# A written order made with other model costs: longer fixed times for VectorE, ScalarE and GpSimd, more time per matmul, a higher backlog limit

## The chip, the cores and the metric

One NeuronCore of a Trainium2 chip runs the whole program. The metric is device microseconds of one execution. The core has TensorE (matmuls and transposes, PE in the profile, with its weight loads under PEld), VectorE (DVE), ScalarE (ACT), GpSimd (POOL) and SyncE (SP, which issues DMAs). Each engine works through its own instructions in the order in which they were written, and waits at semaphores for the others.

## The reference

One layer of a streaming encoder. 1088 tokens (1024 of a new stream and 64 of a running one) of width 1024 pass through:

```
h   = rmsnorm(x) * (1 + sc1) + sh1            # sc, sh, g: silu(c) @ w_ada + b_ada
z   = h @ w_in                                # retention q,k,v,gate; GLA q,k,v,gate; decays
o_r = retention(q, k, v, state)               # 4 heads of 128, chunks with a carried state
o_r = groupnorm(o_r) * g_ret_norm * silu(gate)
o_g = gla(q, k, v, log_a, state)              # 4 heads of 64, decay per channel
o_g = rms(o_g) * g_gla_norm * silu(gate)
x   = x + g1 * (concat(o_r, o_g) @ w_out)
h2  = rmsnorm(x) * (1 + sc2) + sh2
a, up = h2 @ w_ffn_in                         # 2 x 2816
x   = x + g2 * ((silu(conv3(a) + conv_b) * up) @ w_ffn_out);  y = rmsnorm(x)
```

The states of both mixers and the last rows of the convolution are outputs too. All of it is float32.

## The kernel before

Activations lie transposed, with the width on the partitions and tokens along the free axis, in three blocks `c` of 384, 384 and 320 tokens (`CW` is 384, `WID` has the three). The projections of `w_in` (`proj`, `proj2`, `vproj`) are the main work of TensorE. Every operand is split into a high and a low part, and a product is three matmuls: high by high, low by high, high by low (`mm3`, L242). In the trace these main matmuls write tile `mm`, and read `act_hi`, `act_lo` and the split weights `hi`, `lo`. The weight's low part is a VectorE subtraction, `lo<-raw,hi`.

Beside the projections run generators, one for each piece of side work: `gla(p, c0)` for two pairs of GLA heads, `ret(hd, ...)` for four retention heads (L1227), tails that normalize an output (`gla_tail`, `ret_tail`), `decays`, and `mod_pieces`, which computes a part of the modulation on VectorE, ScalarE and GpSimd. Nothing runs them on the chip: they run while the program is written, and so set the order of the instructions. After each triple of main matmuls `flow.tick()` (L124) steps every generator whose time has come. Model time `flow.t` advances only when a matmul or a transpose is written (`mm`, L233, and `tr`, L238). A generator yields the delay after which it wants to go on. Many delays hold `behind()`: each `Engine` (L75 to 98) keeps a model of when it is done, `busy`, to which every operation adds a fixed time and its elements over a rate, and `behind()` is how far that lies ahead of model time. So larger costs of an engine make a generator that waits for it wait for more main matmuls.

Where a stage must be over before the next may begin, `flow.drain` or `flow.until` advance model time without main matmuls: what side work is left then is written with nothing of the projections in between.

A GLA chunk of a pair of heads is: score matmuls of the block itself (`sc<-q,k`, on VectorE `att`), seven levels (operands `qbd` and `kk` from VectorE, ScalarE and GpSimd, one group of score matmuls, and VectorE's sum into `att`), a transpose of `kh`, and three output steps (`o<-...`, state update `sbd` on VectorE). Three chunks follow each other for each pair. Its tail takes sums of squares, a root on VectorE, a scale `on` on ScalarE, and transposes.

A retention chunk is: three score matmuls, `ratt` (VectorE's mask), a transpose of k scaled on ScalarE to `kz`, three output steps (with VectorE's new state `rstate`, the sum `on` and its statistics), and its tail: `rsqrt_steps` (L329, eleven small VectorE instructions `ri`, `rj`, `ra`, `rr`), the scale `on<-on,bmv,rr`, three transposes `sc<-ident,on`, and the product into `mix`. Head 3's gate projection is the last one of the attention. As its blocks finish, `split_mix(c)` (L1346) splits the eight `mix` tiles of block c for the output projection: ScalarE casts `act_hi`, and GpSimd and VectorE subtract `act_lo` by turns. The output projection writes tile `dX`, and VectorE takes it up in `ab`.

`mod_piece` (L529) goes on only when `V.behind()` is not over `VECTOR_LIMIT`:

```
while V.behind() > VECTOR_LIMIT or S.behind() > SCALAR_LIMIT:
    yield 0.3
```

Of the kernel before, what the change touches and what calls it, by code (L numbers as in the profile page):

```python
# [13 lines left out]
F32R = mybir.dt.float32r  # L14
# [50 lines left out]
LOADS_AT = 9.0  # L65
RET_TAIL = 1.0
GLA_TAIL = 2.0
VECTOR_LIMIT = 1.0
SCALAR_LIMIT = 2.0
LEVEL_LIMIT = 1.0  # L70
OUT_LIMIT = 1.0
# [122 lines left out]
def stream_step_kernel(  # L194
# [7 lines left out]
    nc = tc.nc  # L202
    ctx.enter_context(tc.manual_schedule())
    flow = Flow()
    T = nc.tensor
    V = Engine(flow, nc.vector, 960.0, 0.08)
    S = Engine(flow, nc.scalar, 1200.0, 0.09)
    G = Engine(flow, nc.gpsimd, 470.0, 0.09)

    const = ctx.enter_context(tc.tile_pool(name="const", bufs=1))  # L210
    act_ctx, early_ctx, psum_ctx = ExitStack(), ExitStack(), ExitStack()
# [14 lines left out]
    ones = const.tile([P, 1], F32, name="ones")  # L226
    G.memset(ones, 1.0)

# [4 lines left out]
    def mm(out, lhsT, rhs, start, stop, more=False):  # L233
        T.matmul(out, lhsT, rhs, start=start, stop=stop, skip_group_check=more)  # L234
        n = int(np.prod(rhs.shape[1:]))
        flow.t += max(n / 2400 + 0.0025, 0.108) if rhs.dtype == F32R else max(n / 600, 0.213)

    def tr(out, in_, n=P):  # L238
        T.transpose(out=out, in_=in_, identity=ident[0:n, 0:n])
# [2 lines left out]
    def mm3(out, trip, first=True, last=True, tick=True):  # L242
        n = len(trip)
        for i, (sh, sl, mh, ml) in enumerate(trip):
            mm(out, sh, mh, first and i == 0, False)
            mm(out, sh, ml, False, False)
            mm(out, sl, mh, False, last and i == n - 1)
            if tick and i < n - 1:
                flow.tick()
# [27 lines left out]
    def split_unit():  # L277
# [4 lines left out]
        lo = wp.tile([P, nk, ncol], F32R, tag="lo", name="lo", bufs=3)  # L282
        S.copy(out=hi, in_=raw)

        def low(eng=V):
            eng.tensor_tensor(out=lo, in0=raw, in1=hi.bitcast(F32), op=ALU.subtract)
            used[0] = True
# [41 lines left out]
    def rsqrt_steps(v, n, tag, out, w=P):  # L329
        ii = smallp[0].tile([P, n], I32, tag=tag + "i", name=tag + "i", bufs=2)[0:w]  # L330
        V.tensor_scalar(out=ii, in0=v.bitcast(I32), scalar1=1, scalar2=None,
                        op0=ALU.logical_shift_right)
        yield
        jj = smallp[0].tile([P, n], I32, tag=tag + "j", name=tag + "j", bufs=2)[0:w]
        V.tensor_scalar(out=jj, in0=ii, scalar1=-1, scalar2=0x5F3759DF,
                        op0=ALU.mult, op1=ALU.add)
        r = jj.bitcast(F32)
        for it in range(3):
            V.busy += 0.36
            yield  # L340
            a = smallp[0].tile([P, n], F32, tag=f"{tag}a", name=tag + "a", bufs=2)[0:w]
            V.scalar_tensor_tensor(out=a, in0=v, scalar=-0.5, in1=r, op0=ALU.mult, op1=ALU.mult)
            yield
            V.tensor_tensor(out=a, in0=a, in1=r, op=ALU.mult)
            yield
            r2 = smallp[0].tile([P, n], F32, tag=f"{tag}r", name=tag + "r", bufs=3)[0:w]
            V.scalar_tensor_tensor(out=r2, in0=a, scalar=1.5, in1=r, op0=ALU.add, op1=ALU.mult)
            r = r2
        out.append(r)

    def rsqrt(v, n, tag, w=P):
        out = []
        for _ in rsqrt_steps(v, n, tag, out, w):
            pass
        return out[0]
# [12 lines left out]
    def load_x(t):  # L368
# [3 lines left out]
        else:  # L372
            G.memset(xt[SMP:P, :], 0.0)
            nc.sync.dma_start(out=xt[0:SMP, :], in_=x_sample[0])
# [14 lines left out]
    for i, (name, src, n) in enumerate((  # L389
# [3 lines left out]
        if i % 2 == 0 and i < 6:  # L393
# [8 lines left out]
    T.transpose(out=pv[:, 0:16], in_=cr, identity=ident[0:16, 0:16])  # L402
    S.activation(out=csil.rearrange("p k j -> p j k"),
                 in_=pv[:, 0:16].rearrange("p (j k) -> p j k", j=2), func=AF.Silu)
# [41 lines left out]
    def norm_sum(c, j):  # L446
        if c not in ssqs:
            ssqs[c] = small.tile([P, 3], F32, tag="ssq", name="ssq", bufs=3)
        junk = qkp.tile([P, D], mybir.dt.bfloat16, tag="gt", name="junk", bufs=2)
        S.activation(out=junk, in_=xs[c * 3 + j], func=AF.Square, accum_out=ssqs[c][:, j:j + 1])  # L450

    def norm_steps(c):
        vv = small.tile([P, 3], F32, tag="vv", name="vv", bufs=3)
        V.tensor_scalar(out=vv, in0=ssqs[c], scalar1=1.0 / D, scalar2=EPS, op0=ALU.mult,
                        op1=ALU.add)
        out = []
        yield
        yield from rsqrt_steps(vv, 3, "n", out)
        rstds[c] = out[0]

    def norm_scale(c, j, eng):
        x, r = xs[c * 3 + j], rstds[c][:, j:j + 1]
        if eng is S:
            S.activation(out=x, in_=x, func=AF.Copy, scale=r)
        else:
            eng.tensor_scalar(out=x, in0=x, scalar1=r, scalar2=None, op0=ALU.mult)

    c4 = const.tile([P, KD, 4], F32R, name="c4")
    S.copy(out=c4[:, :, 0:2], in_=csil)
    V.tensor_tensor(out=c4[:, :, 2:4], in0=csil, in1=c4[:, :, 0:2].bitcast(F32), op=ALU.subtract)  # L470
# [58 lines left out]
    def mod_piece(which, dst, q, loads):  # L529
        accs = [attn.tile([P, 512], F32, tag=f"acc{j}", name=f"acc{j}", bufs=1) for j in range(2)]  # L530
        for kk in range(0, KD, 2):
# [3 lines left out]
            for i in range(2):  # L535
                for j in range(2):
                    while V.behind() > VECTOR_LIMIT or S.behind() > SCALAR_LIMIT:
                        yield 0.3
                    if j and phase[0] == "ret":
# [3 lines left out]
                        else:  # L543
                            pr = qkp.tile([P, 512], F32, tag="gt", name="prod", bufs=2)
                            S.activation(out=pr, in_=raw[:, i, :], func=AF.Copy,
                                         scale=csil[:, kk + i, 1:2])
                            G.tensor_tensor(out=accs[1], in0=accs[1], in1=pr, op=ALU.add)
                    else:
# [88 lines left out]
    def h_hi(c, k):  # L637
        h[c][k] = act_pair()
        S.copy(out=h[c][k][0], in_=hw[c, k])

    def h_lo(c, k, eng):
        hh, hl = h[c][k]
        eng.tensor_tensor(out=hl, in0=hw[c, k], in1=hh.bitcast(F32), op=ALU.subtract)

    def make_h(c, k):
        h_turn(c, k)
        h_mod(c, k, V)
        h_hi(c, k)
        h_lo(c, k, G)

# [29 lines left out]
    def ev_gla(p, name, scale):  # L680
# [3 lines left out]
        def f(c, w, ps):  # L684
            t = slots.get()
            if w < CW:
                G.memset(t[:, w:CW], 0.0)
            S.mul(out=t[:, 0:w], in_=ps[:, 0:w], mul=scale)
# [3 lines left out]
    def gate_gla(m):  # L692
        def f(c, w, ps):
# [7 lines left out]
            else:  # L701
                V.scalar_tensor_tensor(out=gt[:, 0:w], in0=gt[:, 0:w], scalar=1.0,
                                       in1=ps[:, 0:w], op0=ALU.add, op1=ALU.mult)
                G.tensor_tensor(out=mt[:, 0:w], in0=mt[:, 0:w], in1=gt[:, 0:w], op=ALU.mult)
        return f
# [414 lines left out]
    def gla_tail(p, c, on, ss):  # L1120
        w = WID[c]
        ms = small.tile([P, 6], F32, tag="ms", name="ms", bufs=2)
        V.tensor_scalar(out=ms, in0=ss, scalar1=1.0 / P, scalar2=EPS, op0=ALU.mult, op1=ALU.add)
        rs = []
        for _ in rsqrt_steps(ms, 6, "g", rs):
            yield 0.2
        rs = rs[0]
        yield 0.2
        for j in range(3):
            for hd in range(2):  # L1130
                i = 2 * j + hd
                S.activation(out=on[:, j, hd, :], in_=on[:, j, hd, :], func=AF.Copy,
                             scale=rs[:, i:i + 1])
        yield max(S.behind(), 0.0) + GLA_TAIL
        for hd in range(2):
            pt = bank(ps_sc, "sc")
            for j in range(3):
                tr(pt[:, j * P:(j + 1) * P], on[:, j, hd, :])
            m = 2 * p + hd
            mt = mix[c][4 + m]  # L1140
            if mt is None:
                mt = mix[c][4 + m] = mxg.tile([P, CW], F32, tag="mx", name="mix", bufs=12)
                S.activation(out=mt[:, 0:w], in_=pt[:, 0:w], func=AF.Copy, scale=ghalf[:, m:m + 1])
            else:
                V.scalar_tensor_tensor(out=mt[:, 0:w], in0=pt[:, 0:w], scalar=ghalf[:, m:m + 1],
                                       in1=mt[:, 0:w], op0=ALU.mult, op1=ALU.mult)
            if hd == 1:
                ons.free()
            yield 1.0
# [1211 lines left out]
```

## Time and profile before

| what | us |
|---|---|
| median of 3 runs (1485.37 to 1487.78) | 1486.16 |
| profiled execution | 1485.04 |
| its span | 1483.2 |
| start of the GLA stage, of retention, of the output projection | about 105, 331, 600 |
| TensorE busy | 1364.4 (92% of the span) |
| VectorE busy | 1071.6 (72%) |
| ScalarE, GpSimd busy | 625.4 (42%), 308.9 (21%) |
| mean granted clock of TensorE | 0.979 of full speed |

The profile lists busy time, and for an engine's idle time the work that ended it. A window row gives the busy time of each engine in a stretch of the span, with the number of instructions, and the granted clock: 1.00 is 2.4 GHz, 0.50 is 1.2 GHz. In a row of waits stand the waiting group, the releaser, the sum, the number and the largest. Nearly every side operation is recorded at line 91 (the `Engine` helper) and every matmul at 234 or 239, so groups are told apart by the names of their tiles.

### The profile page before, as it was taken

Reading aid. Unit: us, or ns where it says so; the run is one execution under the profiler, and the core shown is the slowest. Engines: PE = TensorE matmul, PEld = TensorE weight load, DVE = VectorE, ACT = ScalarE, POOL = GpSimd, SP = SyncE. Lnnn points to the kernel's source line nnn. Section 1 sums busy time; section 2 is a strip of 40 time slices with the busy share of each in tenths; the row PEclk is TensorE's granted clock in tenths of the full one; section 3 lists DMA queues with packets and bytes.
Section 4 is the critical chain, followed back from the end, with each engine's and each line's share of the span. In section 5 each row is a group of like instructions: output and inputs, shape, how many; then the busy total and the mean of one; then the engine's idle time right before and its main releaser. Section 6 shows DMA issues by size and latency. Waiting matters only on the chain.

```text
span 1483.2 us, 23803 instructions
## 1 busy us (share of the span) xinstructions
PE 1364.4 (92%) x9082; PEld 1270.0 (86%) x9082; DVE 1071.6 (72%) x1992; ACT 625.4 (42%) x1277; POOL 308.9 (21%) x412
## 2 busy tenths in 40 slices
PE   5998888989989998899779999999999999899996
PEld 3788777879989998899779999999999997788875
DVE  6637878966886788756697777777777765568775
ACT  5635434432333223545454444444434444334343
POOL 3334433425342423411101000000000011100010
PEclk9999999999999999999889999999999999999999
DMA  8420102123223222444212332233223338555522
GB/s 261 150 78 2 58 15 64 57 85 101 90 73 90 81 68 74 139 139 145 81 39 83 107 101 61 83 107 107 93 93 107 107 112 283 189 196 184 174 78 114
DMA packets 157977, 158.27 MB, mean 107 GB/s; under 512 B 9738, under 2 KB 128616, under 8 KB 157864
## 3 DMA queue, kind: packets, MB, share of 16 engines
q1 hardware_dynamic: 147303, 120.58, 26.4%
q0 software_dynamic: 10560, 36.18, 7.0%
q8 instruction: 71, 1.16, 0.3%
q14 instruction: 43, 0.34, 0.1%
HBM read 126.80 MB, written 29.93 MB: 106 GB/s over the span
## 4 chain that ended last, share of the span: by engine, by line
PE 53%; DVE 23%; issue 8%; ACT 7%; DMA 2%; POOL 1%; DVEq 0%; ACTq 0%; POOLq 0%
PE dX L234 22%; PE mm L234 10%; PE dA L234 8%; PE mn L234 5%; PE al L234 3%; PE o L234 2%; DVE lo L91 2%; DMA rb<-d_y 2%; DVE qbd L91 2%; DVE att L91 2%; ACT hi L91 2%; DVE ab L91 1%; DVE acc L91 1%; DVE cv L91 1%; DVE X L91 1%
## 5 line engine op out<-in xcount | busy, mean ns | idle before, releaser
L234 PE MATMUL dX<-X,lo 128*128 128x272 f32 x1344 | 180.8, 290 | 4.8 <-DVE ab L91 2.1
L234 PE MATMUL dX<-X,hi 128*128 128x272 f32 x1296 | 175.2, 292 | 6.1 <-DVE ab L91 2.7
L234 PEld LDWEIGHTS dX<-X,lo 128*128 128x128 f32 x1344 | 174.2, 190 | 6.2 <-ACT X L91 2.1
L234 PEld LDWEIGHTS dX<-X,hi 128*128 128x128 f32 x1296 | 169.1, 191 | 6.9 <-issue 2.9
L234 PE MATMUL mm<-act_hi,hi 128*128 128x384 f32 (+1 forms) x480 | 170.7, 356 | 0.3 <-DVE mix L91 0.2
L234 PE MATMUL mm<-act_lo,hi 128*128 128x384 f32 (+1 forms) x480 | 158.8, 331 | 0.1
L234 PE MATMUL mm<-act_hi,lo 128*128 128x384 f32 (+1 forms) x480 | 158.4, 330 | 0.0
L91 ACT CAST hi<-raw 128x512 fp32r<-128x512 f32 (+1 forms) x116 | 91.1, 787 | 78.5 <-DVE raw L91 66.9
L234 PE MATMUL al<-ba,hi 128*128 128x512 f32 x396 | 101.7, 400 | 4.5 <-DVE x L91 4.5
L234 PE MATMUL mn<-lo,hi 128*128 128x512 f32 x396 | 94.8, 396 | 2.7 <-ACT lo L91 2.1
L234 PEld LDWEIGHTS mm<-act_hi,hi 128*128 128x128 f32 x480 | 92.0, 192 | 1.9 <-DVE mix L91 0.5
L234 PEld LDWEIGHTS mm<-act_lo,hi 128*128 128x128 f32 x480 | 91.9, 191 | 0.7 <-POOL act_lo L91 0.3
L234 PEld LDWEIGHTS mn<-lo,hi 128*128 128x128 f32 x396 | 74.8, 190 | 19.4 <-ACT lo L91 2.6
L234 PEld LDWEIGHTS mm<-act_hi,lo 128*128 128x128 f32 x480 | 91.3, 190 | 0.0
L91 DVE SCALAR_TENSOR_TENSOR cv<-ab,cw,cv 128x1088 f32<-128x1088 f32 x44 | 59.3, 1348 | 44.3 <-ACT cv L91 44.3
L234 PEld LDWEIGHTS al<-ba,hi 128*128 128x128 f32 x396 | 71.9, 190 | 19.6 <-DVE x L91 5.6
L234 PE MATMUL mm<-hi,act_hi 128*128 128x256 f32 x288 | 87.3, 303 | 0.2 <-ACT hi L91 0.2
L234 PE MATMUL mm<-lo,act_hi 128*128 128x256 f32 x288 | 82.1, 285 | 2.5 <-DVE lo L91 2.5
L234 PE MATMUL mm<-hi,act_lo 128*128 128x256 f32 x288 | 81.6, 283 | 0.0
L91 POOL TENSOR_TENSOR acc<-acc,prod 128x512 f32<-128x512 f32 x42 | 64.3, 1530 | 78.2 <-ACT prod L91 77.4
L234 PE MATMUL dX<-act_hi,hi 128*128 128x384 f32 (+1 forms) x192 | 66.6, 347 | 8.8 <-DVE ab L91 4.4
L234 PE MATMUL dA<-X,hi 128*128 128x272 f32 x552 | 74.4, 291 | 0.0
(354 smaller groups left out, 3086.4 us busy)
## 6 DMA issues: line engine op xcount, KB each, us to landing
raw<-in_w_ffn_in_dram SPq DMA_DIRECT2D x44, 512.0 KB, 3.8
raw<-in_w_ada_dram SPq DMA_DIRECT2D x32, 512.0 KB, 4.1
raw<-in_w_in_dram SPq DMA_DIRECT2D x28, 512.0 KB, 3.7
rw<-in_w_ffn_out_dram SPq DMA_DIRECT2D x51, 256.0 KB, 3.4
d_y<-cv POOLq DMA_DIRECT2D x22, 512.0 KB, 4.9
rb<-d_y POOLq DMA_DIRECT2D x44, 256.0 KB, 3.8
raw<-in_w_out_dram SPq DMA_DIRECT2D x18, 512.0 KB, 4.3
wa<-in_w_ada_dram SPq DMA_DIRECT2D x16, 512.0 KB, 5.0
```

Source lines behind the costliest of these rows:

```text
L91: return call(*args, **kw)
L234: T.matmul(out, lhsT, rhs, start=start, stop=stop, skip_group_check=more)
```

## The change

The model costs of the engines are raised (fixed time of an operation from 0.08 to 0.25 us on VectorE, from 0.09 to 0.2 on ScalarE and GpSimd), a matmul is taken to last 0.011 us longer in the fast form (unless it is at the floor of 0.108) and 0.222 at least in the other, the extra 0.36 in the root's steps is taken out, and the limit of VectorE's backlog for `mod_piece` is 1.5 instead of 1.0. None of these lines issues anything; they set the order in which the rest is written.

```diff
-VECTOR_LIMIT = 1.0
+VECTOR_LIMIT = 1.5
...
-    V = Engine(flow, nc.vector, 960.0, 0.08)
-    S = Engine(flow, nc.scalar, 1200.0, 0.09)
-    G = Engine(flow, nc.gpsimd, 470.0, 0.09)
+    V = Engine(flow, nc.vector, 960.0, 0.25)
+    S = Engine(flow, nc.scalar, 1200.0, 0.2)
+    G = Engine(flow, nc.gpsimd, 470.0, 0.2)
...
     def mm(out, lhsT, rhs, start, stop, more=False):
...
-        flow.t += max(n / 2400 + 0.0025, 0.108) if rhs.dtype == F32R else max(n / 600, 0.213)
+        flow.t += max(n / 2400 + 0.0135, 0.108) if rhs.dtype == F32R else max(n / 600, 0.222)
...
         for it in range(3):
-            V.busy += 0.36
             yield
```

The order is the same up to about 105 us, and again from the output projection's normalization on. Three places show what moves between.

TensorE, third chunk of the second GLA pair, from its fifth level to the first output step, before (`sc<-qbd,kk` are the levels, `mm` the main matmuls, `sc<-ident,on` transposes of an earlier chunk's output):

```order
L234 MATMUL sc<-qbd_1077,kk 128x128 x3
L239 MATMUL sc<-ident,on 128x128 x3
L234 MATMUL mm<-act_hi,hi 128x384
L234 MATMUL mm<-act_lo,hi 128x384
L234 MATMUL mm<-act_hi,lo 128x384
L234 MATMUL sc<-qbd_1079,kk 128x128 x3
L234 MATMUL mm<-act_hi,hi 128x384
L234 MATMUL mm<-act_lo,hi 128x384
L234 MATMUL mm<-act_hi,lo 128x384
L234 MATMUL o<-sbd_1083,qe 128x256
L234 MATMUL o<-v,att 128x128 x2
L234 MATMUL o<-v,khT 128x256
```

The same place after:

```order
L234 MATMUL sc<-qbd_1077,kk 128x128 x3
L239 MATMUL sc<-ident,kh 128x128 x3
L239 MATMUL sc<-ident,on 128x128 x6
L234 MATMUL sc<-qbd_1079,kk 128x128 x3
L234 MATMUL sc<-qbd_1075,kk 128x128 x3
L234 MATMUL sc<-qbd_1077,kk 128x128 x3
L234 MATMUL sc<-qbd_1079,kk 128x128 x3
L234 MATMUL o<-sbd_1083,qe 128x256
L234 MATMUL o<-v,att 128x128 x2
L234 MATMUL o<-v,khT 128x256
```

No main matmul is left between the levels and output steps there; they stand in the chunk before, which has 159 of them instead of 108.

VectorE, retention head 1, last output steps of its second chunk, before (`on<-on,bmv,rr` is the scale of the first chunk's output):

```order
L91 SCALAR_TENSOR_TENSOR rstate<-rstate,o 128x128
L91 SCALAR_TENSOR_TENSOR on<-o,txi,on 128x128
L91 BN_STATS bst<-on 128x6
L91 BN_AGGR bmv<-bst 128x2
L91 SCALAR_TENSOR_TENSOR ra<-ve,rr 128x3
L91 SCALAR_TENSOR_TENSOR acc_4357<-raw,csil,acc_4357 128x512
L91 TENSOR_TENSOR ra<-ra,rr 128x3
L91 SCALAR_TENSOR_TENSOR rr<-ra,rr 128x3
L91 TENSOR_TENSOR ratt<-sc,tdec 128x384
L91 TENSOR_SCALAR on<-on,bmv,rr 128x128 x3
```

The same place after:

```order
L91 SCALAR_TENSOR_TENSOR ra<-ve,rr 128x3
L91 TENSOR_TENSOR ra<-ra,rr 128x3
L91 SCALAR_TENSOR_TENSOR rr<-ra,rr 128x3
L91 TENSOR_SCALAR on<-on,bmv,rr 128x128 x3
L91 TENSOR_TENSOR lo<-raw,hi 128x1024
L91 SCALAR_TENSOR_TENSOR rstate<-rstate,o 128x128
L91 SCALAR_TENSOR_TENSOR on<-o,txi,on 128x128
L91 BN_STATS bst<-on 128x6
L91 BN_AGGR bmv<-bst 128x2
L91 TENSOR_REDUCE msum<-st 128x4
L91 TENSOR_TENSOR ratt<-sc,tdec 128x384
```

The scale stands ahead of the third output step instead of behind it, and behind no `ratt`.

VectorE, end of the attention, from the last head's last output step on, before (`rstate<-smp,o` is the last state, `msum` belongs to the modulation):

```order
L91 SCALAR_TENSOR_TENSOR rstate<-smp,o 128x128
L91 SCALAR_TENSOR_TENSOR on<-o,txi,on 128x128
L91 BN_STATS bst<-on 128x6
L91 BN_AGGR bmv<-bst 128x2
L91 TENSOR_TENSOR lo<-raw,hi 128x1024
```

The same place after:

```order
L91 TENSOR_TENSOR act_lo<-mix,act_hi 128x384 x4
L91 SCALAR_TENSOR_TENSOR rstate<-smp,o 128x128
L91 SCALAR_TENSOR_TENSOR on<-o,txi,on 128x128
L91 BN_STATS bst<-on 128x6
L91 BN_AGGR bmv<-bst 128x2
L91 SCALAR_TENSOR_TENSOR mix<-sc,v_122,mix 128x384
L91 TENSOR_SCALAR ve<-bmv 128x3
L91 TENSOR_SCALAR ri<-ve 128x3
L91 TENSOR_SCALAR rj<-ri 128x3
L91 TENSOR_TENSOR act_lo<-mix,act_hi 128x384 x4
```

The subtractions `act_lo` of the first two blocks now stand around the last output step and ahead of the rest of its tail; before they follow the tail's scale. On TensorE 9 main matmuls lie between the last output step with its transposes and the tail's transposes, where there were 51.

## Rows read from the trace of the kernel before

**Rows 1.** The page: busy time, share of the span and instructions of each engine.

```profile
PE 1364.4 (92%) x9082; PEld 1270.0 (86%) x9082; DVE 1071.6 (72%) x1992; ACT 625.4 (42%) x1277; POOL 308.9 (21%) x412
```

**Rows 2.** Windows of GLA and retention: busy by engine, granted clock, DMA share.

```profile
core 0: us, PE busy (x) PEld busy (x) DVE busy (x) ACT busy (x) POOL busy (x), PEclk, DMA share, GB/s
130.00:331.00 201.00, 170.95 (x1157) 156.20 (x1156) 166.86 (x343) 80.67 (x269) 76.75 (x81) 0.98 0.17 51
331.00:592.00 261.00, 240.22 (x1653) 234.14 (x1652) 199.81 (x491) 81.10 (x156) 93.95 (x74) 0.99 0.27 82
```

**Rows 3.** Waits of TensorE, 130 to 331 us: sum, number, largest.

```profile
PE sc L234 <- DVE att L91: 14.3, 13, 3.7
```

**Rows 4.** Waits of TensorE, 331 to 592 us.

```profile
PE sc L239 <- DVE on L91: 10.2, 5, 3.1
PE o L234 <- DVE rstate L91: 4.7, 5, 1.5
PE o L234 <- DVE ratt L91: 3.7, 3, 1.4
```

**Rows 5.** Windows of level stretches, first and last of six.

```profile
137.50:158.70 21.20, 18.79 (x120) 18.22 (x120) 19.55 (x32) 7.70 (x20) 12.28 (x12) 0.92 0.16 46
291.40:313.00 21.60, 17.49 (x114) 15.49 (x113) 19.01 (x41) 7.54 (x22) 9.91 (x10) 1.00 0.05 19
```

**Rows 6.** Windows of whole GLA chunks, the last the stage's tail.

```profile
137.30:167.10 29.80, 26.39 (x169) 24.76 (x170) 25.22 (x45) 11.39 (x37) 12.28 (x12) 0.94 0.18 55
197.90:230.90 33.00, 28.40 (x197) 25.68 (x196) 28.84 (x58) 14.52 (x47) 13.36 (x16) 1.00 0.16 50
230.90:259.60 28.70, 23.73 (x174) 22.39 (x172) 23.07 (x51) 9.62 (x35) 10.91 (x13) 0.94 0.09 26
259.60:289.00 29.40, 26.74 (x196) 24.62 (x195) 26.41 (x55) 13.53 (x47) 11.63 (x12) 1.00 0.17 53
289.00:318.40 29.40, 24.88 (x161) 22.02 (x161) 23.90 (x50) 11.83 (x39) 9.91 (x10) 1.00 0.06 20
318.40:330.70 12.30, 9.93 (x63) 9.03 (x62) 7.73 (x22) 5.26 (x17) 2.46 (x2) 1.00 0.81 248
```

**Rows 7.** Windows of main matmuls; the second counts tile `mm` on TensorE alone.

```profile
114.60:132.30 17.70, 17.70 (x147) 17.62 (x147) 10.53 (x13) 13.10 (x28) 9.91 (x12) 1.00 0.00 1
...
318.40:330.70 12.30, 7.51 (x45) 1.00 0.81 248
```

**Rows 8.** Timeline of TensorE, retention: start, length, operation, idle before.

```profile
394.79 0.50 PE L239 MATMUL sc<-ident,on 128*128 128x128 f32 x2 [2.35 <-DVE on L91]
...
446.94 0.30 PE L239 MATMUL sc<-ident,on 128*128 128x128 f32 x1 [3.10 <-DVE on L91]
...
528.26 0.66 PE L239 MATMUL sc<-ident,on 128*128 128x128 f32 x2 [3.08 <-DVE on L91]
```

**Rows 9.** Timeline of TensorE, end of the attention and output projection.

```profile
586.61 0.38 PE L234 MATMUL o<-smp,q 128*128 128x128 f32 x2
...
613.14 0.69 PE L234 MATMUL dX<-act_hi,hi 128*128 128x384 f32 x1 [4.06 <-DVE ab L91]
```

**Rows 10.** Timeline of VectorE, end of the attention.

```profile
588.57 0.28 DVE L91 SCALAR_TENSOR_TENSOR rstate<-smp,o 128x128 f32<-128x128 f32 x1
...
590.00 1.19 DVE L91 TENSOR_TENSOR lo<-raw,hi 128x1024 fp32r<-128x1024 f32 x1
...
593.83 0.86 DVE L91 TENSOR_SCALAR on<-on,bmv,rr 128x128 f32<-128x128 f32 x3
...
596.50 4.92 DVE L91 TENSOR_TENSOR act_lo<-mix,act_hi 128x384 fp32r<-128x384 f32 x4 [0.26 <-ACT act_hi L91]
```

**Rows 11.** VectorE's `act_lo`: shortest, median and longest in ns.

```profile
L91 DVE TENSOR_TENSOR act_lo<-mix,act_hi x12: 479/1287/1372, 596.5 to 610.8; 128x384 fp32r<-128x384 f32 x8, 128x320 fp32r<-128x320 f32 x4
```

**Rows 12.** Windows at half and at full clock.

```profile
527.20:534.00 6.80, 5.74 (x23) 5.58 (x24) 5.23 (x24) 2.06 (x4) 0.00 (x0) 0.50 0.27 83
612.60:619.30 6.70, 6.16 (x19) 6.16 (x20) 4.02 (x5) 3.40 (x5) 1.26 (x2) 0.50 0.94 259
619.40:640.00 20.60, 20.60 (x125) 20.43 (x124) 9.00 (x12) 7.30 (x12) 2.16 (x4) 1.00 0.56 172
```

## The prediction, made before the changed kernel was timed

> **What bounds the kernel now.** I first read the page's busy line: TensorE works 92% of the span, VectorE 72% [rows 1]. What an order of side work can win is therefore the time in which TensorE stands still, plus the time for which its clock is down afterwards. The instructions move only between about 105 us (start of the GLA stage) and the end of the attention near 600 us, so next come the windows of those two stages: TensorE idles 201.00 − 170.95 = 30.1 us in GLA and 261.00 − 240.22 = 20.8 us in retention [rows 2]. The list of waits then says for whom: in GLA first for `att`, the VectorE product of the score matmuls (14.3 us in 13 waits) [rows 3]; in retention for `on`, the normalized head output that must be transposed (10.2), for `rstate`, the carried state (4.7), and for `ratt`, the masked scores (3.7) [rows 4]. The rest there is 2.2 us of small waits.
>
> Idle time of TensorE alone doesn't tell what bounds a GLA chunk. Six chunks have a stretch of seven levels; in the first VectorE is busy 19.55 of 21.20 us, in the last 19.01 of 21.60 [rows 5], 92% and 88%. VectorE sets the pace of these stretches. TensorE fills its waits with main matmuls of the next projection; taking those away doesn't shorten the chunk, and putting more in lengthens it once TensorE becomes the longer of the two. That is the test I put to each chunk of the new order.
>
> Pitches of main matmuls: 147 of 256 columns take 17.70 us, 0.120 each; 45 of 384 and 320 columns take 7.51, 0.167 each [rows 7].
>
> **The change, part by part.** No main or side matmul is added or removed. Higher model costs make the planner believe that VectorE, ScalarE and GpSimd finish later, so a side generator that waits for its engine waits longer in model time, and more main matmuls go out before its next step; the higher matmul cost works against that. `V.busy += 0.36` emits nothing. Five ScalarE instructions fewer and two VectorE more (some `mix` products take another path) cost nothing: both engines have room [rows 2], and at most 1 us if one lands in a wait.
>
> *Term A, GLA.* Main matmuls move between the chunks. The six windows run from one chunk's first score matmul to the next one's [rows 6], the last is the tail of the stage.
> - Pair 1, chunk 1 (259.6 to 289.0): before 84 mains of 256 columns and 24 of 384; after 33 of 256, and 126 of 384 or 320. That is −51 × 0.120 + 102 × 0.167 = +10.9 us on a TensorE busy for 26.74: 37.6 us against a wall of 29.40. TensorE would be the bound: +8.2.
> - Pair 1, chunk 2: 75 mains become 18, so 24.88 − 57 × 0.167 = 15.4 us remain for TensorE, and VectorE's 23.90 at 90% busy make 26.5: −3 against 29.40.
> - Pair 1, chunk 0: 99 mains become 147, +48 × 0.120 = 5.8; 23.73 + 5.8 = 29.5 against 28.70: +0.8.
> - Tail: its 45 mains are gone. Of the 12.30 us I keep 9 for the chain of sums, root, scale and transposes that these mains covered, an estimate between 12.30 (nothing gained) and 12.30 − 7.51 = 4.8: −3.3.
> - Pair 0: chunk 0 gets 4.5 us more mains, 26.39 + 4.5 = 30.9 against 29.80: +1.1. Chunk 2 with its tail has 8.2 us of mains instead of 14.6; VectorE's 28.84 of 33.00 leaves little to shorten: −1.
> - Clock: three stretches (both chunks 2 and the tail) are now thin. What a fall costs is read at the end of the attention, where TensorE did 19 matmuls in 6.70 us at a granted clock of 0.50 and then 125 in 20.60 at 1.00 [rows 12]: 6.70 − 19 × 0.165 = 3.6 us. I take a bit over half of one, +2.
>
> A is +8.2 − 3 + 0.8 − 3.3 + 1.1 − 1 + 2 = **+4.8**. From below −1: VectorE, set free in the long chunk 1, runs ahead into chunk 2's levels and gives the 8.2 back. From above +13: both chunks 2 and the tail run at half clock for most of their length (third rival).
>
> On the clock, after TensorE's wait of 4.06 us [rows 9] the granted clock stood at 0.50, which is 1.2 GHz, from 612.6 to 619.3 [rows 12]. The Trainium skill, "TensorE: Matmul & The Clock Gate", section "HAM oscillation — how this bites in real kernels", says that a pause of the engine throttles it again, so that every pause costs twice; the trace agrees. By that rule each thin stretch would pay, which is the slow rival below; without it the clock's +2 would be 0.
>
> *Term B, retention.* The three `o` steps of a chunk stand 12 mains apart instead of 6, and the scores are 6 instead of 3 mains ahead of `ratt`. Six more mains last 0.7 to 1.0 us; the longest `rstate` wait is 1.5 [rows 4], so of 4.7 us I leave 1.3. Three more last 0.4 to 0.5; of `ratt`'s 3.7 I leave 2.2. The `on` waits are of two kinds. In one the scale of `on` stands behind other VectorE work, and goes where the order places it earlier: in head 1 the scale now precedes the third `rstate` of chunk 1, and the 3.10 at 446.94 go; in head 3 the two small ones go (10.2 less the three of [rows 8], 1.7). In the other the transposes keep their place, as in head 2 (528.26, 3.08) [rows 8]. That stays, its half clock of 527.2 to 534.0 [rows 12] too, and of the 2.35 at 394.79 in head 0 half stays: 4.3 of 10.2 left. With 2.0 of the rest, 9.8 of 20.8 us are left: −11. Moved work starts waits that no row of before shows, and I give 2 for them: **−9**. Bounds: −13 (rows as computed, and half of the staying waits go) and −4 (only the waits that the order visibly undoes).
>
> *Term C, end of the attention.* Before, after the last state matmul at 586.61 TensorE has 51 mains of the last projection to cover VectorE's way to `on` (593.83 + 0.86) [rows 9, 10]; then comes a wait of 4.06 us at the third `dX`, for the subtractions `act_lo` that VectorE still has to do ahead of `ab` [rows 9], and the half clock, 3.6 by the sum above: 7.7 us lost. After, the same mains went out earlier. Behind the state matmul stand the transposes of chunk 1, 9 mains (1.5 us) and then the transposes that need `on`. On VectorE four `act_lo` stand ahead of the `rstate`, and four more between it and the `on`. From the `rstate` on: 588.57 to 590.00, as before, 1.4; `mix` about 0.6 (an estimate: half of the `lo`); four `act_lo` 4.92; `lo` 1.19; from the end of `lo` at 591.19 to the end of `on` at 594.69, 3.5 [rows 10]. Together 11.6, of which 2.6 lie beside TensorE's last matmuls, transposes and mains: 9 us idle. The four `act_lo` ahead of the `rstate` delay it as far as they aren't done when the state matmul ends, between 0 and 4.9; I take 2.5, since ScalarE's casts must come first. Then half clock 3.6, and the later `act_lo` wait is gone, as most subtractions are done. 9 + 2.5 + 3.6 − 7.7 = +7.4, taken as **+7**. Bounds: an `act_lo` took between 0.479 and 1.372 us [rows 11]; at the lowest the four take 1.9 instead of 4.9, and with nothing ahead of `rstate` C is +1; with all four ahead it is +9.
>
> Sum: +4.8 − 9 + 7 = +2.8, some 3 us. On the profiled execution's 1485.04 us (its span of 1483.2 and 1.8 around it) that is 1488. This execution lies 1.1 us under the median of the runs, 1486.16, so I predict **1489.2 us**. With a measurement that can tell about 0.2%, the edges of "no change" are 1483.2 and 1489.1.
>
> **The rivals.**
> 1. *Small loss (forecast)*, 1486 to 1493.
> 2. *Faster.* Only the two visible waits stay (5.4 of 20.8, B = −15.4), and GLA costs nothing, because VectorE keeps its order of work and in the lengthened chunk gets ahead. For it: VectorE's share in the levels. Against it: 37.6 us of TensorE work in one chunk, and VectorE can't get ahead of buffers that TensorE must free. With C = +7: −8, 1478. C's low bound gives 1472.
> 3. *Much slower by the clock.* A thin chunk 2 has 15.4 us of TensorE work; at half clock that is up to 31 us, over the 26.5 of VectorE, +4 each in the two chunks 2, and +2 in the tail. It decides once TensorE's waits for `att` (14.3 / 13 = 1.1 us each, largest 3.7 [rows 3]) grow to the size of the 3 to 4 us that went with a fall. A = +13, sum +11, 1497. Against it: in chunk 1 of pair 1 and in retention the cover grows.
> 4. *No effect.* What one place loses another gives back, since the waits are for VectorE, whose work is the same; the mains only stand elsewhere: 1486.
>
> **How the numbers follow.** Chances: forecast 0.43, faster 0.25, much slower 0.19, no effect 0.13. Slower by over 0.2% is the third and some six tenths of the first: 0.45. Faster is the second and a little of the first: 0.27. The rest, 0.28, is no change. The bounds of the three terms add up to −1 − 13 + 1 = −13 and +13 − 4 + 9 = +18 around the median; all three at one end is unlikely, so I draw both in by 3: 1476 to 1501. The forecast's own range is 1484 to 1494.
>
> **What would show it.** In the profile after: chunk 1 of pair 1 long (36 to 38 us from its first score matmul to the next) with TensorE nearly without idle time and chunk 2 at 26 to 27; a retention stage with 10 to 13 us of waits, the 3.1 for `on` in head 1 gone; TensorE idle for 9 us or more right before the first `dX`, and none of 4 us at the third. The forecast is wrong if the long chunk isn't long (A falls away), if the clock falls in more places than before (third rival), or if the transposes at the end find `on` ready (C was mis-sized).

## The result and the profile after

The changed kernel took 1510.03 us (median of 4, 1507.29 to 1511.23) against 1486.97 (median of 4) before. That is 23 us more; the measured ratio, 1.0135 (95% interval 1.0111 to 1.0159), is a little lower than that of these two medians and stands for 20 us. The prediction was 3 us more, with a range up to 1501. The first view is the busy line of the page, beside that of before [rows 1].

```profile
PE 1377.3 (91%) x9082; PEld 1284.7 (85%) x9082; DVE 1069.5 (71%) x1994; ACT 622.5 (41%) x1272; POOL 302.9 (20%) x410
```

The engines do the same work. TensorE's busy time grew by 12.9 us with not one matmul more, so a part of it ran at a lower clock (0.959 on the mean, 0.979 before); the rest of the 26.3 us between the two spans is idle time.

Marks that both traces have show where the time went (us from the span's start):

| mark on TensorE | before | after | difference |
|---|---|---|---|
| first score matmul of the GLA stage | 132.35 | 135.53 | +3.2 |
| of pair 0, chunk 2 | 196.29 | 198.96 | +2.7 |
| of pair 1, chunk 0 | 228.69 | 236.42 | +7.7 |
| of pair 1, chunk 1 | 259.63 | 271.83 | +12.2 |
| of pair 1, chunk 2 | 289.05 | 311.92 | +22.9 |
| last state matmul of GLA | 318.42 | 344.66 | +26.2 |
| main matmuls resume, all side work of GLA over | 330.71 | 354.72 | +24.0 |
| last state matmul of retention (`o<-smp,q`) | 586.61 | 612.15 | +25.5 |
| first FFN matmul (`dA`) | 646.79 | 671.31 | +24.5 |
| end of the span | 1483.25 | 1509.47 | +26.2 |

Up to the resumption both have written the same 1056 main matmuls. So term A (GLA) is +24.0 (the expectation of run 1 below has 354.0 and 23.3). From there to the last state matmul the changed kernel does 57 main matmuls more, 1287 against 1230: 42 of 384 and 15 of 320 columns, about 9.5 us at the 0.167 of [rows 7]. So B is 257.4 − 9.5 = 247.9 against 255.9, −8.0. From that to the first FFN matmul it does 57 fewer (9 instead of 66, of which 51 lay ahead of the tail's transposes and 15 behind them): 59.2 + 9.5 = 68.7 against 60.2, C = +8.5. The last 1.7 us lie in the FFN, where the order is the same; I have no cause for them.

Windows of the changed kernel: the six GLA chunks, each from its first score matmul on, retention, the end of the attention (columns as in [rows 2]).

```profile
135.53:164.40 28.87, 28.87 (x194) 28.05 (x193) 22.44 (x42) 10.55 (x33) 11.65 (x12) 1.00 0.19 56
164.40:198.96 34.56, 29.51 (x169) 27.23 (x169) 23.70 (x52) 12.36 (x43) 11.72 (x13) 0.85 0.10 31
198.96:236.42 37.46, 27.30 (x152) 23.94 (x151) 28.15 (x59) 14.45 (x49) 10.55 (x13) 0.77 0.18 55
236.42:271.83 35.41, 31.43 (x241) 30.15 (x240) 26.06 (x56) 11.40 (x40) 13.92 (x16) 0.95 0.08 24
271.83:311.92 40.09, 37.15 (x247) 35.34 (x246) 32.55 (x63) 16.49 (x54) 14.80 (x14) 1.00 0.18 53
311.92:344.66 32.74, 22.56 (x104) 19.28 (x104) 20.26 (x45) 9.07 (x31) 8.39 (x8) 0.69 0.11 33
...
354.00:592.00 238.00, 227.44 (x1549) 223.07 (x1550) 182.31 (x420) 73.81 (x142) 89.95 (x73) 0.97 0.28 84
592.00:630.00 38.00, 22.32 (x154) 21.73 (x153) 33.40 (x91) 16.08 (x40) 14.59 (x13) 0.84 0.24 69
```

Read the last chunk: VectorE, which I had taken for its pace, was busy 20.26 of 32.74 us, 62%; TensorE's granted clock was 0.69. In the chunk before it TensorE was busy 37.15 of 40.09.

Waits of TensorE in the changed kernel's retention, 354 to 592 us, against [rows 4] (one more for `ratt`, of 1.2, follows before the last state matmul):

```profile
PE sc L239 <- DVE on L91: 4.6, 4, 2.1
PE o L234 <- DVE ratt L91: 3.8, 4, 1.6
PE o L234 <- DVE rstate L91: 1.6, 2, 1.2
```

And the end of the attention on TensorE, against [rows 9]: the one large wait now stands ahead of the last transposes.

```profile
612.15 0.38 PE L234 MATMUL o<-smp,q 128*128 128x128 f32 x2
...
629.13 0.90 PE L239 MATMUL sc<-ident,on 128*128 128x128 f32 x3 [14.50 <-DVE on L91]
629.68 0.67 PE L234 MATMUL dX<-act_hi,hi 128*128 128x384 f32 x1
```

### The profile page after: what moved, and what is told of

Its sections match the earlier page's. It is cut to its first block, busy times and chain, and to the rows that moved or that the text cites. A ratio compares the mean times of both kernels' runs of the same rounds, so it can differ in the third digit from the quotient of the medians.

```text
span 1509.5 us, 23791 instructions
## 1 busy us (share of the span) xinstructions
PE 1377.3 (91%) x9082; PEld 1284.7 (85%) x9082; DVE 1069.5 (71%) x1994; ACT 622.5 (41%) x1272; POOL 302.9 (20%) x410
## 4 chain that ended last, share of the span: by engine, by line
PE 61%; DVE 19%; ACT 6%; issue 6%; DMA 2%; POOL 0%; SPq 0%; DVEq 0%; ACTq 0%; POOLq 0%
PE dX L234 22%; PE mm L234 16%; PE dA L234 8%; PE mn L234 5%; PE al L234 3%; PE o L234 3%; DVE lo L91 3%; PE sc L234 2%; DVE acc L91 2%; DMA rb<-d_y 2%; ACT hi L91 1%; DVE ab L91 1%; DVE cv L91 1%; DVE X L91 1%; ACT cv L91 1%
## 5 line engine op out<-in xcount | busy, mean ns | idle before, releaser
L91 DVE SCALAR_TENSOR_TENSOR cv<-ab,cw,cv 128x1088 f32<-128x1088 f32 x44 | 59.2, 1346 | 43.7 <-ACT cv L91 43.7
L91 DVE TENSOR_TENSOR lo<-raw,hi 128x1024 fp32r<-128x1024 f32 x43 | 55.5, 1294 | 28.5 <-ACT hi L91 28.4
L91 POOL TENSOR_TENSOR acc<-acc,prod 128x512 f32<-128x512 f32 x42 | 59.1, 1406 | 78.1 <-ACT prod L91 76.2
```

The costliest lines, as they stand in the source:

```text
L91: return call(*args, **kw)
```

## The experiments

All start from the kernel before. A helper `costs(ops, mm)` switches the model: `ops` the three fixed times, the root's extra and the limit of the modulation pieces, `mm` the matmul's time. Called as `costs(1, 1)` at the start it writes the changed kernel's order.

**1. New costs from retention on alone.**

```diff
-    phase[0] = "ret"
+    phase[0] = "ret"; costs(1, 1)
```

> The old model costs up to the end of the GLA stage, the new ones from retention on. Theory (nearly all of the loss is in GLA: the main matmuls resume 23.3 us later after it, at 354.0 against 330.7, and are 24.5 us late at the first FFN product): 1486 to 1490 us, about 1 over before. Rival (the loss comes as much from retention and the end of the attention, which only inherit another supply of main matmuls): 1495 to 1500.

1.0075 (1.0054 to 1.0097), some 11 us over: the rival's side, though not for its reason. By the start of head 3 this kernel was 13.7 us *ahead* of before; between the last state matmul and the first output product it lost 27, though it had 51 main matmuls fewer to do there. TensorE's largest wait there:

```profile
PE st L239 <- DVE acc L91: 22.0, 1, 22.0
```

`acc` is the modulation. Eight of its accumulations were written after the last head, where `flow.drain(pieces)` has nothing to put beside them. With longer model times VectorE is "behind" more often, a limit of 1.5 holds the pieces back, and here they didn't end in time. In the changed kernel they do: by the start of head 3 it has written 77 of VectorE's 80 accumulations, this run 68, though both had written 40 by retention's first score matmul. Why the same costs hold the pieces back in one and not in the other isn't shown.

**2. The complement: new costs in GLA alone.**

```diff
+    costs(1, 1)
...
-    phase[0] = "ret"
+    phase[0] = "ret"; costs(0, 0)
```

> The complement: new costs up to the end of GLA, old ones from retention on. Theory: the whole GLA loss and nothing else, 1487 + 23 = 1510 us (1506 to 1513). Rival (loss spread over both): 1497 or less. If this and the other half add up to the whole change, the parts don't depend on each other.

1.0149 (1.0125 to 1.0172), 1510.7 us: the order of GLA alone brings the whole loss. The halves don't add up to the change, though (11 + 22 against 23): the first half has the left-over pieces, which the whole has not.

**3 and 5. The thin chunks filled.** The changed kernel; `FILL` stands for the numbers by pair and chunk that the expectations give.

```diff
             fin(c, o)
+            fb = bank(ps_st, "st") if (p, c) in FILL else None
+            for _ in range(FILL.get((p, c), 0)):
+                T.matmul(fb[:, 0:P], ident, ident, start=True, stop=True)
```

> The changed kernel with idle matmuls of the identity (written to a free bank, read by nobody) behind every score and output group of the thin GLA chunks: 3 in pair 0 chunk 1, 6 in pair 0 chunk 2 and in pair 1 chunk 2. They add work to TensorE and take no wait away. Theory (the clock falls because TensorE stands still between the groups, and the half clock makes these chunks long): no half clock in those three chunks, which were 34.6, 37.4 and 32.8 us and become about 31, 32 and 28; time 1510 - 12 = 1498 (1493 to 1502). Rival (the chunks are long because the waits are no longer covered, whatever the clock): 1510 to 1514, the added matmuls either in the waits or on top.

> The fill of identity matmuls with half the dose: 3 instead of 6 behind every group in pair 0 chunk 2 and pair 1 chunk 2, 1 instead of 3 in pair 0 chunk 1. Six lasted 1.50 us and with them TensorE was busy 37.48 of 39.30 us in the thinnest chunk, so the fill itself had become the bound and that run could not decide. Three last 0.75. Theory (clock): full clock in the three chunks and TensorE no longer the bound; they become about 31, 32 and 28 us instead of 34.6, 37.4 and 32.8, time 1497 to 1502. Rival (missing cover: what is left is the way score group, VectorE, next group, whatever the clock): 1507 to 1512 even at full clock.

Full dose 1.0158 (1.0131 to 1.0184), half dose 1.0139 (1.0096 to 1.0182): no time back in either. Windows of the half dose, from first score matmul to first score matmul or last state matmul, for the three chunks that were 34.6, 37.5 and 32.7 at clocks of 0.85, 0.77 and 0.69:

```profile
165.48:200.03 34.55, 30.47 (x196) 28.43 (x195) 23.93 (x52) 12.56 (x44) 11.71 (x13) 0.95 0.10 31
200.03:238.28 38.25, 32.48 (x230) 30.04 (x229) 27.67 (x59) 14.19 (x49) 10.19 (x13) 0.91 0.17 53
314.56:347.29 32.73, 26.89 (x176) 24.81 (x176) 20.53 (x45) 8.96 (x30) 8.40 (x8) 0.84 0.12 34
```

The clock came back for the most part (with the full dose wholly), and no chunk got shorter. That doesn't clear the clock. The chain of work that ended last, which the profile follows back from the last instruction, runs through the fills themselves: for 24.8 us of the three chunks with the full dose and for 12.0 with the half. What the clock gave back, the fills could take.

**4 and 6. New costs for retention heads 0 to 2, with the pieces' limit at 1.5 and at 2.5.**

```diff
-    phase[0] = "ret"
+    phase[0] = "ret"; costs(1, 1); model.limit = 2.5    # run 4 without the limit
...
-    r3 = flow.start(ret(3, C_RV + 256, P, True))
+    costs(0, 0); r3 = flow.start(ret(3, C_RV + 256, P, True))
```

> New costs for retention heads 0 to 2 alone, old ones before and after. Theory (the new spacing of side steps gains about 4 us in retention, read between the end of GLA and the start of head 3, and the end of the attention, which loses 5, keeps its cover of main matmuls): 1483 us (1480 to 1485), faster than before. Rival (the gain is only main matmuls that came from the GLA stage's tail): 1486 to 1488.

> New costs in retention heads 0 to 2 alone, as before, but with the backlog limit of the modulation pieces at 2.5 there instead of 1.5. Theory (with long model times and a limit of 1.5 the pieces fell behind, and the last one was written after the attention with nothing beside it: 22 us of idle TensorE before the first output product; the new spacing itself had gained 12 us by the start of head 3): all pieces end within the attention, none of the 22 us, 1475 to 1481 us, under before. Rival (the 12 us were only the pieces' VectorE work put off): 1486 to 1490.

1.0111 (1.0085 to 1.0136), and with the higher limit 0.9963 (0.9947 to 0.9979): one number, 1.5 or 2.5, is worth 20 us here. Run 4 missed its 1483 for the reason of run 1 (26.4 us of wait for `acc`). Run 6 is faster than before, by 5 us (1483.7, where 1475 to 1481 was expected); the new spacing does help retention once the pieces keep up.

**7. Fixed times between old and new** (0.16; 0.136; root's extra 0.12; rest as changed).

> Everything as changed, but fixed times between the old and the new ones: 0.16 on VectorE, 0.136 on ScalarE and GpSimd, 0.12 in the root's steps. Theory (the loss in GLA comes from fixed times that overshoot the traced operations, so that a chunk of 29 us is planned with 38 us of TensorE work and the supply of main matmuls runs out): the long chunk has 17.4 us of main matmuls instead of 24.8 and stays under VectorE's time; GLA loses at most 3 us, total 1484 to 1490. Rival (any longer times do it): 1498 or more.

1.0082 (1.0059 to 1.0106): the rival's side. About half the overshoot, half the loss.

**8 and 9. The end of the attention in another order.** Run 8 writes the subtractions of blocks 1 and 2 behind the last tail, block 0's on GpSimd; run 9 is run 8 with all of them on VectorE.

```diff
-            (V if i % 2 else G).tensor_tensor(out=ml[:, 0:w], in0=mix[c][k][:, 0:w],
+            (V if i % 2 and c else G).tensor_tensor(out=ml[:, 0:w], in0=mix[c][k][:, 0:w],    # run 8
+            V.tensor_tensor(out=ml[:, 0:w], in0=mix[c][k][:, 0:w],                            # run 9
...
-        if c and ready[nsp] == RH:
+        if c and not nsp and ready[nsp] == RH:
...
-    release()
+    release(); flow.drain(r3, *tails_)
```

> The changed kernel with another order at the end of the attention alone: the subtractions of block 0 all on GpSimd, those of blocks 1 and 2 written behind the last tail's scale and transposes, so that none stands on VectorE ahead of them. Theory (the 14.5 us that TensorE idles before the first output product are the two groups of four subtractions, 4.9 and 4.1 us, that VectorE does first, plus small operations slowed beside GpSimd): the idle time falls to 4 to 6 us, the time by 6, to 1504 (1501 to 1507). Rival (the subtractions only move: the output products wait for them instead): 1508 to 1511.

1.0120 (1.0097 to 1.0143): between theory and rival by the time, and by the trace a miss, since TensorE still idled 13.03 us at the same place. No subtraction stood ahead of `on` on VectorE any more. VectorE's root steps on 128 x 3 elements did, and GpSimd beside them (two steps, and GpSimd's 16 subtractions in 15.81 us):

```profile
616.73 0.93 DVE L91 SCALAR_TENSOR_TENSOR rr<-ra,rj 128x3 f32<-128x3 f32 x1
617.69 0.92 DVE L91 SCALAR_TENSOR_TENSOR ra<-ve,rr 128x3 f32<-128x3 f32 x1
```

```profile
607.98 15.81 POOL L91 TENSOR_TENSOR act_lo<-mix,act_hi 128x384 fp32r<-128x384 f32 x16 [16.68 <-ACT act_hi L91]
```

Each small step waited about as long as one subtraction of GpSimd lasts (15.81 / 16 = 0.99). That made run 9.

> The changed kernel with all 24 subtractions of the attention's end on VectorE and none on GpSimd; block 0 stays where it was, blocks 1 and 2 are written behind the last tail. In the run before this one VectorE's root steps on 128 x 3 elements took 0.78 to 0.93 us each while GpSimd subtracted, 0.16 without it. Theory (the two engines shut each other out of the memory while GpSimd subtracts, so its cheap help is what makes the end long): root steps of 0.16, subtractions of 0.48 or less, TensorE idle 6 to 8 us instead of 14.5 before the first output product, time 1.0135 - 0.005 = 1.0085 of before (1.006 to 1.010). Rival (small operations are slow there for another reason, and VectorE with twice the subtractions takes longer): 1.013 or more.

1.0075 (1.0045 to 1.0105), 0.6% under the whole change. TensorE's wait, a root step, and the 24 subtractions (shortest, median, longest in ns) of run 9:

```profile
620.26 0.90 PE L239 MATMUL sc<-ident,on 128*128 128x128 f32 x3 [6.04 <-DVE on L91]
```

```profile
616.95 0.16 DVE L91 SCALAR_TENSOR_TENSOR ra<-ve,rj 128x3 f32<-128x3 f32 x1
```

```profile
L91 DVE TENSOR_TENSOR act_lo<-mix,act_hi x24: 480/550/559, 610.7 to 628.2; 128x384 fp32r<-128x384 f32 x16, 128x320 fp32r<-128x320 f32 x8
```

All 24 keep VectorE busy for 10.9 us. Before, the 12 of [rows 11] kept it busy for 13.6 beside GpSimd's 14.4 for the other 12.

**10 and 11. The same subtractions on VectorE in run 6's kernel, and in the kernel before.**

> The version with new costs in retention heads 0 to 2 and the backlog limit of 2.5, which ran at 0.9963 of before, with all subtractions of the attention's end on VectorE. Theory (memory shared with GpSimd): 4 to 7 us less, 0.992 to 0.9935 of before. Rival: 0.996 or more.

> The kernel before with nothing changed but these 24 subtractions, all on VectorE. Before, VectorE took 13.6 us for 12 of them beside GpSimd's 14.4 for the other 12, and the third output product waited 4.06 us with a half clock behind it. Theory: 24 take 11 to 12 us on VectorE alone, the wait of 4.06 and the half clock go, 0.995 to 0.998 of before. Rival: twice the subtractions make VectorE later, 1.000 or more.

0.9935 (0.9914 to 0.9957) and 0.9971 (0.9950 to 0.9993), both as expected; in run 11 TensorE's wait of 4.06 us for `ab` [rows 9] is 0.2. Run 10, 1477.7 us against 1489.0 before on the same chip, is the best version found: new costs in three retention heads, a limit of 2.5, no subtraction on GpSimd.

**12. A GLA chunk with no cover at all.**

```diff
+            if (p, c, o) == (1, 2, "diag"):
+                flow.alone = lambda: g1[2]     # the next tick runs the pair to its end
             fin(c, o)
...
```

> The kernel before, old costs, with the 75 main matmuls (12.3 us) of the last GLA chunk written behind it, so that the chunk has none; nothing else of that chunk changes its order. It asks how long a chunk without cover takes. My prediction's step (a thin chunk goes on at VectorE's pace, 90% busy): 26 to 27 us from its first score matmul to its last state update instead of 29.4, time about 9 us over before. Theory now (the chunk is a chain from GpSimd, ScalarE and VectorE to TensorE and back, with little to spare, and TensorE's main matmuls fitted into its gaps at no cost): 29 to 33 us, the main matmuls come on top, 12 to 16 us over before.

1.0035 (1.0016 to 1.0055), 4 to 5 us over, under both. The chunk, from its first score matmul to its last state matmul:

```profile
290.54:319.07 28.53, 17.41 (x87) 14.75 (x86) 24.47 (x48) 10.55 (x34) 9.58 (x10) 0.70 0.19 56
```

Without one main matmul, and at a clock of 0.70, it took 28.53 us against 29.37. Two things changed at once, and their effects can cancel: the run bounds their sum and doesn't say what either is worth. It does show that a chunk without cover can be shorter than the changed kernel's 32.74 at 0.69. The main matmuls came on top (10.0 us late at retention's first score matmul); by the medians about half of that was given back later.

**13 to 15. Which costs make GLA long.** New costs in GLA alone, as in run 2, with the two limits of levels and output steps at 2.0 (13), for ScalarE and GpSimd alone (14), for VectorE alone (15).

```diff
-LEVEL_LIMIT = 1.0
-OUT_LIMIT = 1.0
+LEVEL_LIMIT = 2.0     # run 13, with model.limit = 2.5 from retention on
+OUT_LIMIT = 2.0
...
+    costs(1, 1); V.fixed = 0.08; model.step = 0.36; model.limit = 1.0    # run 14
+    costs(1, 1); S.fixed = 0.09; G.fixed = 0.09                          # run 15
```

> New costs in GLA, old ones from retention on, as in the run that took 1.0149 of before, but with the two other backlog limits of GLA raised like the third: levels and output steps may be 2.0 behind instead of 1.0 (and the modulation pieces 2.5 from retention on, so that none is left over). The supply of main matmuls becomes even: 15.4, 15.4 and 14.9 us in the three chunks of pair 1 instead of 17.2, 24.8 and 2.6. Theory (with longer model times the old limits hold the levels back for main matmuls that the chip doesn't need, until they run out): GLA at most 4 us longer than before, 0.997 to 1.003 of before. Rival (the order inside the chunks is worse however the main matmuls are spread): 1.008 or more.

> New fixed times for ScalarE and GpSimd alone in GLA (VectorE's and the root's old, backlog limit old, the matmul's cost new), all old from retention on. Main matmuls of pair 1's chunks: 14.7, 17.3, 12.2 us. Theory (it is the uneven supply, and VectorE's time makes that): at most 6 us over before, 0.998 to 1.004. Rival (ScalarE and GpSimd hold the levels back, as the limit is on them): 1.008 or more.

> New fixed time for VectorE alone in GLA (ScalarE and GpSimd old; root's extra out, limit 1.5, matmul's cost new), all old from retention on. Main matmuls of pair 1's chunks: 16.8, 22.9, 5.6 us, nearly those of the whole change. Theory (uneven supply through VectorE): most of the 22 us, 1.009 to 1.014 of before. Rival: 1.005 or less.

1.0227 (1.0202 to 1.0253), 1.0074 (1.0046 to 1.0102), 1.0068 (1.0044 to 1.0093): three misses. At the first score matmul of retention they were 11.4, 16.3 and 15.8 us late, run 2 24.8. So either group of engines alone makes two thirds of the loss, and the higher limits take away half. Even that half isn't shown to be the supply's: in run 13 only 17 of VectorE's modulation accumulations ran in the GLA chunks, against 31 before and 32 after. The 14 others came due in retention, where this kernel lost 28 us more.

What the GLA chunks of all these runs say together (main matmuls written in the chunk, worked out from the pitches; length; granted clock):

| kernel | pair 1, chunk 1 | pair 1, chunk 2 |
|---|---|---|
| before | 14.0: 29.4, 1.00 | 12.3: 29.4, 1.00 |
| 12 | 14.0: 29.4, 1.00 | none: 28.5, 0.70 |
| 13 | 15.4: 32.5, 1.00 | 14.9: 38.0, 0.87 |
| 14 | 17.3: 34.3, 1.00 | 12.2: 32.7, 0.90 |
| 7 | 17.4: 35.7, 1.00 | 11.8: 27.3, 1.00 |
| 15 | 22.9: 37.3, 1.00 | 5.6: 30.3, 0.83 |
| after | 24.8: 40.1, 1.00 | 2.6: 32.7, 0.69 |

Chunk 1 grows with its main matmuls; chunk 2 follows neither them nor the mean clock alone.

## Why the prediction was wrong

**Term A failed**, +24.0 measured against +4.8. By its own steps: the long chunk 1 of pair 1 was right in kind and nearly in size (+8.2; 29.4 to 40.1 is +10.7, with TensorE busy 93% at full clock). The tail was right in kind (−3.3; 12.3 to 10.1). Chunk 0 of pair 0 with what lies before it came out at −1.1 (+1.1). What failed is the step for thin chunks, "VectorE's time at 90% busy", together with the +2 for the clock: pair 1's last chunk −3, measured +3.4; pair 0's with its tail −1, measured +5.1. Pair 0's chunk 1, for which the sum has no term and [rows 6] no row, grew by 3.7, and pair 1's chunk 0 by 4.5 (+0.8). These four make 16.7 us against −3.2, and −1.2 with the clock's +2. (Three rows of [rows 6] begin 1.6 to 5 us behind the first score matmul: by the marks the chunks 0 and 2 of pair 0 and 0 of pair 1 lasted 33.1, 32.4 and 30.9 us before.)

The step takes a chunk as the longer of two sums, TensorE's and VectorE's, so that a slower matmul costs nothing as long as VectorE has more to do. In the trace of the changed kernel the two take turns. The last output steps of pair 1's last chunk stand on the chain of work that ended last, `o` on TensorE, then `sbd` on VectorE, then `o`. The `o` groups there after, at a granted clock of 0.50 (1.2 GHz), and in run 12, at 1.00:

```profile
337.35 2.09 PE o L234 x6
340.24 5.05 PE o L234 x16
```

```profile
314.81 1.16 PE o L237 x6
316.78 2.89 PE o L237 x16
```

The same 22 matmuls take 7.1 us instead of 4.1 (before 4.1 too), and that is most of the 4.2 us by which this chunk is longer than run 12's at the same mean clock. Over the whole chunk the pieces of the chain say (us; the loss is an estimate: each TensorE piece's length times the share of the clock that was missing):

| pair 1's last chunk | length | TensorE on the chain | of it lost to the low clock | VectorE on the chain |
|---|---|---|---|---|
| before | 29.4 | 6.4 | 0 | 16.6 |
| after | 32.7 | 16.1 | 7.3 | 9.8 |
| run 12 | 28.5 | 9.6 | 3.1 | 14.5 |
| run 5 | 32.7 | 18.7 (6.6 fills) | 4.4 | 8.9 |
| run 3 | 33.9 | 21.9 (12.3 fills) | 0 | 7.2 |

The same estimate gives 16.1 us for the four chunks that grew, and 1.7 before: some 14 us of low clock where the prediction has 2. It is an upper bound, as other work may end last once the matmuls are faster. No run has these chunks thin and at full clock without added matmuls, so the clock's share is read from the chain and not shown by an experiment; without it they would have grown by 2 us or more instead of 16.7.

I had read VectorE's 88 to 92% in the level stretches [rows 5] as a throughput that the work could always reach. It was reached with the order before. The start of pair 1's last chunk shows what the order itself adds. VectorE before, whose chunk's scores began at 289.05 (`att` takes them up):

```profile
290.01 0.71 DVE L91 TENSOR_TENSOR qbd<-q,dd 64x192 f32<-64x192 f32 x2
290.94 0.55 DVE L91 SCALAR_TENSOR_TENSOR gt<-gt,mm 128x384 f32<-128x384 f32 x1 [0.22 <-ACT gt L91]
291.42 1.05 DVE L91 COPY_PREDICATED att<-tmask,sc 128x384 f32<-128x384 int32 x2
```

VectorE after, whose scores began at 311.92:

```profile
312.85 0.56 DVE L91 SCALAR_TENSOR_TENSOR mix<-gt,mm 128x384 f32<-128x384 f32 x1 [0.94 <-ACT gt L91]
313.33 1.22 DVE L91 TENSOR_TENSOR lo<-raw,hi 128x1024 fp32r<-128x1024 f32 x1
314.46 0.96 DVE L91 TENSOR_SCALAR gj<-gi 128x6 int32<-128x6 int32 x1
315.34 0.55 DVE L91 TENSOR_TENSOR kk<-k,dd 128x384 f32<-128x384 f32 x1
315.81 0.71 DVE L91 TENSOR_TENSOR qbd<-q,dd 64x192 f32<-64x192 f32 x2
...
316.63 1.04 DVE L91 COPY_PREDICATED att<-tmask,sc 128x384 f32<-128x384 int32 x2
```

`att` comes 4.7 us after its scores began instead of 2.4, and the first level's `qbd` 3.9 instead of 1.0: a gate product that waits for ScalarE, a weight's low part and a slow root step stand ahead of them. These 2.3 us are argued from one chunk's rows; which rule of the planner writes it so stays open (runs 14 and 15: no single engine's cost, run 13: the limits on levels and outputs in part).

**The third rival**, slower by the clock, came nearest in time (1497), named both chunks 2, and had the nearest cause: the granted clock fell from 1.00 to 0.69 and 0.77 there, as it said. It gave them +4 each, since it too took the longer of two sums (TensorE at half clock, 31 us, over VectorE's 26.5). By the rule cited from the Trainium skill, "TensorE: Matmul & The Clock Gate", section "HAM oscillation — how this bites in real kernels", each pause costs twice. The trace of the changed kernel agrees: a wait of 3.10 us for `att`, then six score matmuls at 0.50 in 1.62 us, where before six behind a wait took 0.95 at 1.00. I had named a clock that falls in more places than before as a sign that the forecast is wrong, and it did fall (0.959 on the mean instead of 0.979).

**Term B** was right in mechanism and size, −8.0 against −9. The waits for `on` fell from 10.2 to 4.6 (I left 4.3) and for `rstate` from 4.7 to 1.6 (1.3); `ratt` rose from 3.7 to 5.0 (2.2). In all TensorE stands still for 11.8 us of this stretch instead of 20.8 (I left 9.8, and 2 for new waits), and about 1 us went into a clock of 0.97 instead of 0.99 [rows 2]. From the resumption to the start of head 3 the changed kernel gains 5.3 us, run 6 8.0, and runs 1 and 4 13.0 and 11.8, part of it the pieces put off.

**Term C** was right, +8.5 against +7: TensorE idle for 14.5 us against 11.5 worked out, and no wait at the third `dX`. I took `mix` to `rj` at their lone durations, and after they weren't alone:

```profile
611.48 4.90 DVE L91 TENSOR_TENSOR act_lo<-mix,act_hi 128x384 fp32r<-128x384 f32 x4 [0.62 <-ACT act_hi L91]
616.31 0.27 DVE L91 SCALAR_TENSOR_TENSOR rstate<-smp,o 128x128 f32<-128x128 f32 x1
...
618.76 0.92 DVE L91 TENSOR_SCALAR ri<-ve 128x3 int32<-128x3 int32 x1
619.71 0.92 DVE L91 TENSOR_SCALAR rj<-ri 128x3 int32<-128x3 int32 x1
620.54 4.09 DVE L91 TENSOR_TENSOR act_lo<-mix,act_hi 128x384 fp32r<-128x384 f32 x4
...
626.61 0.16 DVE L91 TENSOR_TENSOR ra<-ra,rr 128x3 f32<-128x3 f32 x1
```

B and C were right, and so was their sum (−2, measured +0.5); the miss is A's alone. Its upper bound, +13, was too low by 11, because the bound too took the longer of the two sums for the thin chunks.

## What to carry to other kernels

A busy share of 90% belongs to the order that reached it: when the order changes, bound a stage by the chain through its engines, not by the busiest engine's sum, and where cover is taken away price the matmuls on that chain at the lower clock (22 of them took 7.1 us instead of 4.1). A fill that is to bring the clock back can cost on the chain what it gains. When a planner's costs go up, every limit that is compared with them is part of the change, and what falls behind such a limit ends up where nothing covers it (22 us in run 1, 20 us between 1.5 and 2.5). Before an elementwise job is shared between VectorE and GpSimd, time it on VectorE alone.

## What the runs showed of the hardware

Beside GpSimd's subtractions with two operands in SBUF, VectorE took 0.92 us instead of 0.16 for steps on 128 x 3 elements, and a median of 1.29 us [rows 11] instead of 0.55 for a subtraction of its own. The Trainium skill, "SBUF — State Buffer", section "Who interferes with whom", says that VectorE's instructions with two SBUF inputs and GpSimd's reads share one pair of ports under an exclusive lock, so that one waits for the whole of the other; the traces of runs 8 and 9 agree, at 0.99 us for one GpSimd subtraction. The `ri` and `rj` steps have a single tensor input and were held up just as long (0.92).
